# Low parts of key and value weights by subtraction on VectorE, pooling sums emitted between keys and values, late modulation moved among the pairs and behind the weighted scores

## The chip, the cores and the metric

The kernel runs on one core of one Trainium2 chip. The metric is the device time of one execution in microseconds (us). The kernel before takes 945.13 us, the median of three runs (944.65 to 946.53).

A core has engines that run in parallel, each with its own in-order list of instructions: TensorE (PE in the profile; its weight loads are PEld) multiplies matrices, VectorE (DVE) and ScalarE (ACT) work on vectors, GpSimd (POOL) does little arithmetic here but issues some transfers, and SyncE (SP) issues the other transfers. Transfers (DMA) move data between the large memory and the on-chip memory. One engine waits for another, or for a transfer, through semaphores.

## The reference

One layer of a hybrid diffusion backbone, for 512 latent tokens and 256 context tokens of width 1024, all in float32:

```
mod = silu(c) @ w_ada + b_ada            # six rows: shift, scale, gate, twice
a   = rmsnorm(x) * norm * (1 + scale1) + shift1      # latent and context tokens
p   = a @ w_in                           # pooling input u, q, k, v, output gate, two branch gates, 16 mLSTM gates
pool = ((window_mean(u, 2/4/8/16) - u) @ w_pool[g]) * pool_scale       # four groups, on an 8 x 64 grid
q, k = silu(short_conv(q, k))            # three taps along the tokens
h    = mlstm(q, k, v, gates) forward + backward      # four heads of 256, chunks of 128, start state from the context
m    = rmsnorm(h) * gain * sigmoid(o)
y    = sigmoid(g5) * pool + sigmoid(g6) * m
x    = x + gate1 * (y @ w_out)
x    = x + gate2 * swiglu(rmsnorm(x) * norm * (1 + scale2) + shift2)
out  = rmsnorm(x) * norm
```

The last four rows of `mod` (gate1, shift2, scale2, gate2) are needed only from `y @ w_out` on.

## The kernel before

**How a product is made.** A float32 matrix is held as two matrices of type float32r: a high part (the value rounded by a cast) and a low part (the value minus the high part). `mm3` (L186) forms each product from three matmuls, high by high (L190), high by low of the activations (L191), low of the weights by high (L192). Every weight that is used has to be loaded, cast (ScalarE) and given a low part before L192 can run. `wload` (L150) does this: it loads the weight into a staging tile `wr` (three buffers), casts it to `wh` on ScalarE (L156) and makes `wl`. `wh` and `wl` have two buffers each, so the cast of one weight waits until the matmuls of the weight two before have read theirs.

**Two ways to the low part.** With no destination given, VectorE subtracts: `wl = wr - wh` (L158). With the destination `"added"`, ScalarE writes the negated weight, rounded, into `wl` (L160), and GpSimd then issues a second transfer of the same weight out of the large memory, which adds it onto `wl` on its way (L161). `keys(h)` for heads 1 to 3 (L591) and `values(h)` for heads 1 to 3 (L711, through `vload`, L194) take this second way: two weights of 512 KB each per call, twelve in all. The pooling pairs and the feed-forward have a similar transfer of their own (L238), which the change leaves alone.

**The stages.** The first 60 us prepare modulation and the normed tokens `aT` and `acT`. Then values of head 0, and the stage of the pairs (`Pool`, a subclass of `Seven`): eight times a pair of 128-column weight blocks, the pooling input and its gate, is multiplied by seven products in place of eight. Its step for pair j has a `front`, in which four of the products run, a `prepare` of pair j+1, which loads two weight blocks (`wr`, `ur`) and forms sums and low parts, and a `back` for pair j-1. `back` calls `later` and `done`, which store results (`td`, `ud`) for later use.

Then the four heads. For each head h the order in the program before is: (from head 1 on) `values(h)`, `attention(h)`, `queries(h+1)`, the rest of attention, `both_pooled(h)`, `keys(h+1)`, `mixed(h)`. For the last head `both_pooled(3)` stands ahead of `values(3)`. `attention` runs twice (two halves of the latent tokens) through `scores` (L938: products of keys and queries, weighted by decays on VectorE and split again into high and low) and `apply` (L978: products of the weighted scores with the values). `pooled` (L603) reads back a pooling input tile (`pa`, one buffer), and sums it over windows by additions on VectorE through `pb` (two buffers), scales by a loaded count table (L639, L643) and subtracts. `pool_mix` (L647) multiplies the result by the pooling weights. `mixed` joins the branches. After head 3 follow the output projection and the feed-forward.

**Late modulation.** The 32 column blocks of `mod` that are needed late are not matmuls. `late_mod(n, behind, among)` (L681) loads n blocks of 512 KB each of `w_ada` and forms each block's sum by one VectorE instruction (L687), which is held in VectorE's order behind a given instruction. With `among` it takes a `wr` buffer, otherwise a `pb` buffer, the ones that `pooled` uses. Before, the 32 blocks stand at: one per pair (8), one behind each token tile of values for heads 1 to 3 (18), and one behind each half of attention in heads 0 to 2 (6).

**What sets the order.** The first stage and part of the feed-forward are ordered by hand. Everywhere else a planner orders each engine's list, from its own cost estimates, and gives earlier places in the program priority. Each engine then runs its list strictly in that order, and so does each queue of transfers: one that waits for a buffer holds back those behind it. PSUM banks for products rotate through four tiles `ps` and four `pat`.

Of the kernel before, what the change touches and what calls it, by code (L numbers as in the profile page):

```python
# [49 lines left out]
def layer_kernel(ctx: ExitStack, tc, xT, cT, w0, w1, wv0, wv, wada_a, wada_b, par, crow, bg, wpool,  # L50
# [99 lines left out]
    def wload(src, n, dst=None, skip=0):  # L150

        raw = tl("wr", [P, WMAX], F32, 3)
        nc.sync.dma_start(raw[:, :n], src)
        if dst is None or dst == "added":
            wh, wl = (tl(t, [P, WMAX], F32R, 2, LINE)[:, skip:skip + n] for t in ("wh", "wl"))
            nc.scalar.copy(wh, raw[:, :n])  # L156
            if dst is None:
                V.tensor_sub(wl, raw[:, :n], wh.bitcast(F32))  # L158
            else:
                nc.scalar.activation(wl, raw[:, :n], AF.Copy, scale=-1.0)  # L160
                nc.gpsimd.dma_start(wl, src, accum_op=ALU.add)  # L161
            return [(wh[:, i * P:(i + 1) * P], wl[:, i * P:(i + 1) * P]) for i in range(n // P)], wh, wl
# [13 lines left out]
        return parts, None, None  # L176

    def split(src, h, l):
        nc.scalar.copy(h, src)  # L179
        V.tensor_sub(l, src, h.bitcast(F32))  # L180
        return h, l
# [11 lines left out]

    def vload(src, n, i, dst=None):  # L194

        _, wh, wl = wload(src[:, i * 4 * n:(i + 1) * 4 * n], 4 * n, dst, min(NEXT, WMAX - 4 * n))
        return [(wh[:, c * n:(c + 1) * n], wl[:, c * n:(c + 1) * n]) for c in range(4)]
# [388 lines left out]
    def keys(h):  # L586
# [3 lines left out]
        for dk in range(2):  # L590
            w = wload(w1[K0 + 2 * h + dk], D, "added" if h else "Sp")[0]  # L591
            acc, acc2 = PS(), PS()
# [115 lines left out]
    def values(h, wp=None):  # L708
        n = DH + NG if h == 0 else DH
        if wp is None:  # L710
            wp = vload(wv[h - 1], n, 0, "added") + vload(wv[h - 1], n, 1, "added")  # L711
        vh = tl("vh", [P, NTOK, DH + 2], F32R)
# [5 lines left out]
        for i, half in ((2, 0), (3, 0), (4, 0), (2, 1), (3, 1), (4, 1), (5, 0), (5, 1), (0, 0), (0, 1), (1, 0), (1, 1)):  # L718
# [15 lines left out]
            nc.scalar.copy(vh[:, i, :DH], acc[:, :DH])  # L734
            low = V.tensor_sub(vl[:, i, :DH], acc[:, :DH], vh[:, i, :DH].bitcast(F32))
            if h:
                late_mod(1, low)
        return vh, vl
# [110 lines left out]
    class Pool(Seven):  # L849
# [6 lines left out]
        def later(self, j, s, y, q):  # L856
            tanh_half(s[:, TC:], y)
            nc.sync.dma_start(td[j], s)
            late_mod(1, self.sub, True)

# [69 lines left out]
    def attention(h, qs, ks, vals, gt, fill):  # L930
# [7 lines left out]
        def scores(th, dec):  # L938
# [3 lines left out]
            for pr in (0, 1, 2):  # L942
# [9 lines left out]
                for d in range(2):  # L952
# [21 lines left out]
                    for e, t, c in where:  # L974
                        parts[d][2 * pr + e][t] = (Sh[:, c:c + P], Sl[:, c:c + P])
            return parts

        def apply(th, parts):  # L978
# [26 lines left out]
            c2 = slice(2 * th, 2 * th + 2)  # L1005
            done = V.tensor_scalar(ss[:, c2], ss[:, c2], 1.0 / DH, EPS, ALU.mult, ALU.add)
# [3 lines left out]
            late_mod((1, 1, 1, 0)[h], done)  # L1010
            return th, hs
# [64 lines left out]
    for h in range(H):  # L1076
        if h == 0:
            k_ = keys(0)
            gt = next(gen)
            q_ = queries(0)  # L1080
        else:
            if h == H - 1:
                pp = both_pooled(h)
            v = values(h)
        rest = attention(h, q_, k_, v, gt, mgate(3 + h))
        if h < H - 1:
            q_ = queries(h + 1)
            rest()
            pp = both_pooled(h)
            k_ = keys(h + 1)  # L1090
        else:
            for n in ("att", "kqp", "vg"):
                close_pool(n)
            open_pool("late1", ("act", "oh", "ol", "gh", "gl"))
            for j in range(6):
                y_split(j)
            mgate_all(KT - 1)
            rest()
# [395 lines left out]
```

## Time and profile before

| | |
|---|---|
| time, median of 3 runs | 945.13 us |
| time of the profiled execution | 946.36 us |
| span of its instructions | 944.5 us |
| TensorE busy, share of the span | 896.0 us, 95% |
| VectorE busy | 633.9 us, 67% |
| ScalarE busy | 485.3 us, 51% |
| GpSimd busy | 93.2 us, 10% |
| mean granted TensorE clock | 0.974 |
| moved by transfers | 141.41 MB, 150 GB/s |
| stage of the pairs | about 70 to 160 us |
| heads | about 160 to 545 us |

The profile is of one execution. Its busy times count instructions that run. A line of a group or of the timeline names engine, source line, operation, the tile written, the tile read, and in square brackets the time that the engine sat idle just before and what ended it. "DMA" is the share of time that the sixteen transfer engines were busy, and "PEclk" the TensorE clock that was granted, as a share of full speed. The chain of waits follows the work that ended last back to its start.

### The profile page before, as it was taken

How to read it: one execution, taken by the hardware profiler on the slowest of the kernel's cores; microseconds unless marked ns; L12 is line 12 of the kernel's file. 1: busy time of each engine (PE TensorE's matmuls, PEld its weight loads, DVE VectorE, ACT ScalarE, POOL GpSimd, SP SyncE). 2: the span in 40 equal slices, each digit the busy share in tenths (PEclk: the TensorE clock that was granted, in tenths of full speed). 3: DMA queues.
4: the chain of work that ended last, by engine and by line, in shares of the span. 5: the costliest groups of instructions: out<-in, count | busy, mean ns of one | idle time of the engine just before them, and what ended most of it. 6: DMA issues, size and time to landing. Idle time of an engine off the chain costs nothing.

```text
span 944.5 us, 16003 instructions
## 1 busy us (share of the span) xinstructions
PE 896.0 (95%) x6218; PEld 823.1 (87%) x6218; DVE 633.9 (67%) x1231; ACT 485.3 (51%) x931; POOL 93.2 (10%) x121
## 2 busy tenths in 40 slices
PE   9999999999889987998779999999999999999997
PEld 7779999888779876997678889999889998899997
DVE  5699874676567755875777577787456754667544
ACT  4576663375354525444444645676234742566542
POOL 0001110011020102011110000011000110111000
PEclk9999999999889988998998999999999999999999
DMA  9747996331666066525553383067236652656502
GB/s 355 304 131 214 284 251 197 122 97 47 163 181 197 24 144 188 182 53 123 132 169 101 120 293 123 24 165 180 80 110 170 159 135 78 177 146 139 135 8 90
DMA packets 58125, 141.41 MB, mean 150 GB/s; under 512 B 13728, under 2 KB 18112, under 8 KB 57024
## 3 DMA queue, kind: packets, MB, share of 16 engines
q1 hardware_dynamic: 48544, 119.93, 39.8%
q0 software_dynamic: 9504, 20.45, 12.5%
q8 instruction: 49, 0.80, 0.3%
q14 instruction: 28, 0.23, 0.1%
HBM read 131.69 MB, written 8.67 MB: 149 GB/s over the span
## 4 chain that ended last, share of the span: by engine, by line
PE 68%; DMA 11%; DVE 9%; issue 6%; ACT 4%; POOL 0%; DVEq 0%; POOLq 0%; SPq 0%; ACTq 0%
PE ps L190 15%; PE ps L192 15%; PE ps L191 15%; DMA pb<-in_wada_b 3%; DMA wl<-in_w 3%; PE pat L190 3%; PE pat L191 3%; PE pat L192 3%; DMA wl<-in_wv 2%; PE pat L492 2%; PE pat L991 1%; PE pat L989 1%; PE pat L990 1%; PE ps L725 1%; DMA E<-rd 1%
## 5 line engine op out<-in xcount | busy, mean ns | idle before, releaser
L156 ACT CAST wh<-wr 128x1024 fp32r<-128x1024 f32 (+3 forms) x62 | 61.8, 1001 | 115.7 <-PE ps L191 97.2
L192 PE MATMUL ps<-a,wl 128*128 128x512 f32 (+1 forms) x240 | 92.5, 385 | 13.2 <-DMA wl<-in_w 13.2
L190 PE MATMUL ps<-a,wh 128*128 128x512 f32 (+1 forms) x240 | 92.4, 385 | 0.0
L191 PE MATMUL ps<-a,wh 128*128 128x512 f32 (+1 forms) x240 | 92.1, 384 | 0.0
L192 PE MATMUL ps<-act,wl 128*128 128x512 f32 (+1 forms) x224 | 78.0, 348 | 0.9 <-DVE wl L158 0.9
L158 DVE TENSOR_TENSOR wl<-wr,wh 128x1024 fp32r<-128x1024 f32 (+3 forms) x50 | 57.5, 1149 | 30.8 <-ACT wh L156 30.0
L190 PE MATMUL ps<-act,wh 128*128 128x512 f32 (+1 forms) x224 | 77.9, 348 | 0.2 <-DVE tmp L1219 0.2
L191 PE MATMUL ps<-act,wh 128*128 128x512 f32 (+1 forms) x224 | 77.8, 347 | 0.1
L192 PEld LDWEIGHTS ps<-a,wl 128*128 128x128 f32 x240 | 48.8, 203 | 21.4 <-DMA wl<-in_w 13.8
L725 PE MATMUL ps<-wl,a 128*128 128x256 f32 (+1 forms) x192 | 56.0, 292 | 9.7 <-DMA wl<-in_wv 8.8
L238 POOL DMA_DIRECT2D ol<-in_wffi x38 | 33.0, 876 | 256.4 <-ACT ol L237 90.3
L179 ACT CAST wh<-sg 128x1024 fp32r<-128x1024 f32 x27 | 28.4, 1051 | 57.9 <-PE pat L191 47.3
L724 PE MATMUL ps<-wh,a 128*128 128x256 f32 (+1 forms) x192 | 55.8, 291 | 1.2 <-DVE tmp L562 1.2
L726 PE MATMUL ps<-wh,a 128*128 128x256 f32 (+1 forms) x192 | 55.5, 289 | 0.0
L190 PEld LDWEIGHTS ps<-a,wh 128*128 128x128 f32 x240 | 48.8, 203 | 6.9
L191 PEld LDWEIGHTS ps<-a,wh 128*128 128x128 f32 x240 | 48.6, 203 | 6.9
L180 DVE TENSOR_TENSOR wl<-sg,wh 128x1024 fp32r<-128x1024 f32 x27 | 33.1, 1224 | 31.6 <-ACT wh L179 31.5
L190 PE MATMUL ps<-hp,gh 128*128 128x256 f32 x176 | 49.9, 283 | 1.0 <-ACT pat L274 1.0
L1342 DVE SCALAR_TENSOR_TENSOR x<-ps,lb,x 128x512 f32<-128x512 f32 (+1 forms) x32 | 19.6, 616 | 45.0 <-PE ps L192 45.0
L190 PE MATMUL ps<-hp,oh 128*128 128x256 f32 x176 | 49.3, 280 | 0.1
L192 PE MATMUL ps<-hp,gl 128*128 128x256 f32 x176 | 49.2, 280 | 0.0
L191 PE MATMUL ps<-hp,gh 128*128 128x256 f32 x176 | 49.1, 279 | 0.0
(368 smaller groups left out, 3063.6 us busy)
## 6 DMA issues: line engine op xcount, KB each, us to landing
wr<-in_w SPq DMA_DIRECT2D x34, 512.0 KB, 3.9
wr<-in_wffi SPq DMA_DIRECT2D x25, 512.0 KB, 4.0
pb<-in_wada_b SPq DMA_DIRECT2D x24, 512.0 KB, 4.3
ur<-in_wffi SPq DMA_DIRECT2D x19, 512.0 KB, 4.1
ol<-in_wffi POOLq DMA_DIRECT2D x38, 256.0 KB, 5.1
ada<-in_wada_a SPq DMA_DIRECT2D x8, 1024.0 KB, 9.3
wr<-in_wffo SPq DMA_DIRECT2D x16, 448.0 KB, 3.8
ur<-in_w SPq DMA_DIRECT2D x8, 512.0 KB, 5.6
```

The source lines that it names most:

```text
L156: nc.scalar.copy(wh, raw[:, :n])
L158: V.tensor_sub(wl, raw[:, :n], wh.bitcast(F32))
L179: nc.scalar.copy(h, src)
L180: V.tensor_sub(l, src, h.bitcast(F32))
L190: nc.tensor.matmul(dst, wh, ah, start=first and i == 0, stop=False, skip_group_check=on)
L191: nc.tensor.matmul(dst, wh, al, start=False, stop=False, skip_group_check=on)
L192: nc.tensor.matmul(dst, wl, ah, start=False, stop=last and i == n - 1, skip_group_check=on)
L238: nc.gpsimd.dma_start(l, dram, accum_op=ALU.add)
L724: nc.tensor.matmul(acc[:, :n], ah, wh, start=kk == 0, stop=False)
L725: nc.tensor.matmul(acc[:, :n], ah, wl, start=False, stop=False)
L726: nc.tensor.matmul(acc[:, :n], al, wh, start=False, stop=kk == KT - 1)
L1342: V.scalar_tensor_tensor(x1[j][:, c], acc[:, c], g2[:, j:j + 1], x1[j][:, c], ALU.mult, ALU.add)
```

## The change

- The `"added"` way is gone from `wload` and `vload`. The twelve weights of keys and values in heads 1 to 3 get their low part by the subtraction on VectorE (L158). Their second transfer and their second ScalarE pass are gone.
- The program's order in the heads: `keys(h+1)`, then `both_pooled(h)`, then `values(h+1)`, then `mixed(h)`. For the last head `both_pooled(3)` stands behind the loads and splits of the stored branches (`y_split`) and ahead of the last gate tile.
- Late modulation: two blocks per pair (16), and two behind each half's weighted scores in all four heads (16), behind the last low part that `scores` makes. None behind the values or behind `apply`.

```
--- before.py
+++ after.py
@@ -151,14 +151,10 @@
 
         raw = tl("wr", [P, WMAX], F32, 3)
         nc.sync.dma_start(raw[:, :n], src)
-        if dst is None or dst == "added":
+        if dst is None:
             wh, wl = (tl(t, [P, WMAX], F32R, 2, LINE)[:, skip:skip + n] for t in ("wh", "wl"))
             nc.scalar.copy(wh, raw[:, :n])
-            if dst is None:
-                V.tensor_sub(wl, raw[:, :n], wh.bitcast(F32))
-            else:
-                nc.scalar.activation(wl, raw[:, :n], AF.Copy, scale=-1.0)
-                nc.gpsimd.dma_start(wl, src, accum_op=ALU.add)
+            V.tensor_sub(wl, raw[:, :n], wh.bitcast(F32))
             return [(wh[:, i * P:(i + 1) * P], wl[:, i * P:(i + 1) * P]) for i in range(n // P)], wh, wl
         if dst == "wide":
             h, l = (wide(t)[:, skip:skip + n] for t in ("gh", "gl"))
@@ -175,9 +171,11 @@
             parts += [(h[:, i * P:(i + 1) * P], l[:, i * P:(i + 1) * P]) for i in range(m // P)]
         return parts, None, None
 
+    low_part = [None]
+
     def split(src, h, l):
         nc.scalar.copy(h, src)
-        V.tensor_sub(l, src, h.bitcast(F32))
+        low_part[0] = V.tensor_sub(l, src, h.bitcast(F32))
         return h, l
 
     def tsplit(src, tag):
@@ -191,9 +189,9 @@
             nc.tensor.matmul(dst, wh, al, start=False, stop=False, skip_group_check=on)
             nc.tensor.matmul(dst, wl, ah, start=False, stop=last and i == n - 1, skip_group_check=on)
 
-    def vload(src, n, i, dst=None):
-
-        _, wh, wl = wload(src[:, i * 4 * n:(i + 1) * 4 * n], 4 * n, dst, min(NEXT, WMAX - 4 * n))
+    def vload(src, n, i):
+
+        _, wh, wl = wload(src[:, i * 4 * n:(i + 1) * 4 * n], 4 * n, skip=min(NEXT, WMAX - 4 * n))
         return [(wh[:, c * n:(c + 1) * n], wl[:, c * n:(c + 1) * n]) for c in range(4)]
 
 
@@ -588,7 +586,7 @@
         ks = []
         kch, kcl = S("kq", F32R), S("kq", F32R)
         for dk in range(2):
-            w = wload(w1[K0 + 2 * h + dk], D, "added" if h else "Sp")[0]
+            w = wload(w1[K0 + 2 * h + dk], D, None if h else "Sp")[0]
             acc, acc2 = PS(), PS()
             mm3(acc[:, :TC], w, acT)
             mm3(acc2, w, aT)
@@ -708,7 +706,7 @@
     def values(h, wp=None):
         n = DH + NG if h == 0 else DH
         if wp is None:
-            wp = vload(wv[h - 1], n, 0, "added") + vload(wv[h - 1], n, 1, "added")
+            wp = vload(wv[h - 1], n, 0) + vload(wv[h - 1], n, 1)
         vh = tl("vh", [P, NTOK, DH + 2], F32R)
         vl = tl("vl", [P, NTOK, DH + 2], F32R)
         nc.gpsimd.memset(vh[:, :, DH:DH + 1].bitcast(F32), 1.0)
@@ -732,9 +730,7 @@
                 for d, j in ((0, i), (1, 1 - i if i < 2 else 7 - i)):
                     V.tensor_add(gif[:, :, d, j, :], gsrc[:, d], bsrc[:, d])
             nc.scalar.copy(vh[:, i, :DH], acc[:, :DH])
-            low = V.tensor_sub(vl[:, i, :DH], acc[:, :DH], vh[:, i, :DH].bitcast(F32))
-            if h:
-                late_mod(1, low)
+            V.tensor_sub(vl[:, i, :DH], acc[:, :DH], vh[:, i, :DH].bitcast(F32))
         return vh, vl
 
 
@@ -856,7 +852,7 @@
         def later(self, j, s, y, q):
             tanh_half(s[:, TC:], y)
             nc.sync.dma_start(td[j], s)
-            late_mod(1, self.sub, True)
+            late_mod(2, self.sub, True)
 
         def done(self, j, s, x, q):
             nc.scalar.copy(q[:, :TC], x)
@@ -973,6 +969,7 @@
                     split(St[:, :n], Sh[:, :n], Sl[:, :n])
                     for e, t, c in where:
                         parts[d][2 * pr + e][t] = (Sh[:, c:c + P], Sl[:, c:c + P])
+            late_mod(2, low_part[0])
             return parts
 
         def apply(th, parts):
@@ -1003,11 +1000,10 @@
                 nc.scalar.activation(hb[:, :DH], hh, AF.Square, accum_out=ss[:, i:i + 1])
                 hs.append(hh)
             c2 = slice(2 * th, 2 * th + 2)
-            done = V.tensor_scalar(ss[:, c2], ss[:, c2], 1.0 / DH, EPS, ALU.mult, ALU.add)
+            V.tensor_scalar(ss[:, c2], ss[:, c2], 1.0 / DH, EPS, ALU.mult, ALU.add)
             nc.gpsimd.tensor_tensor(rst[:, c2], ss[:, c2], mhalf[:, :2], ALU.pow)
             for t in range(2):
                 nc.scalar.activation(hs[t], hs[t], AF.Copy, scale=rst[:, 2 * th + t:2 * th + t + 1])
-            late_mod((1, 1, 1, 0)[h], done)
             return th, hs
 
         def turn(th, hs):
@@ -1078,22 +1074,20 @@
             k_ = keys(0)
             gt = next(gen)
             q_ = queries(0)
-        else:
-            if h == H - 1:
-                pp = both_pooled(h)
-            v = values(h)
         rest = attention(h, q_, k_, v, gt, mgate(3 + h))
         if h < H - 1:
             q_ = queries(h + 1)
             rest()
+            k_ = keys(h + 1)
             pp = both_pooled(h)
-            k_ = keys(h + 1)
+            v = values(h + 1)
         else:
             for n in ("att", "kqp", "vg"):
                 close_pool(n)
             open_pool("late1", ("act", "oh", "ol", "gh", "gl"))
             for j in range(6):
                 y_split(j)
+            pp = both_pooled(h)
             mgate_all(KT - 1)
             rest()
         mixed(h, pp)
```

More of the change, by code (lines that the diff above doesn't have):

```diff
@@ L153, in wload @@
         nc.sync.dma_start(raw[:, :n], src)
-        if dst is None or dst == "added":
+        if dst is None:
             wh, wl = (tl(t, [P, WMAX], F32R, 2, LINE)[:, skip:skip + n] for t in ("wh", "wl"))
             nc.scalar.copy(wh, raw[:, :n])
[L157 to L161, printed above, removed]
+            V.tensor_sub(wl, raw[:, :n], wh.bitcast(F32))
             return [(wh[:, i * P:(i + 1) * P], wl[:, i * P:(i + 1) * P]) for i in range(n // P)], wh, wl
@@ L1088, in layer_kernel @@
             rest()
+            k_ = keys(h + 1)
             pp = both_pooled(h)
-            k_ = keys(h + 1)
+            v = values(h + 1)
         else:
```

26 lines of the change are left out of this document (11 added, 15 removed).

## The prediction

> **What bounds the kernel now.** I read the page first (engines, then the forty slices).
>
> ```profile
> span 944.5 us, 16003 instructions
> PE 896.0 (95%) x6218; PEld 823.1 (87%) x6218; DVE 633.9 (67%) x1231; ACT 485.3 (51%) x931; POOL 93.2 (10%) x121
> ...
> PEclk9999999999889988998998999999999999999999
> DMA  9747996331666066525553383067236652656502
> ```
>
> TensorE sets the time: 95% busy, and its clock dips in slices 11 to 22 alone, the heads. So I asked for the busy times of stretches: the pairs, the heads, then the places behind each long wait.
>
> ```profile
> core 0: us, PE busy (x) PEld busy (x) DVE busy (x) ACT busy (x) POOL busy (x), PEclk, DMA share, GB/s
> 90.00:145.00 55.00, 55.00 (x475) 55.00 (x475) 44.48 (x73) 34.89 (x67) 9.63 (x11) 1.00 0.96 269
> 230.00:500.00 270.00, 233.83 (x1417) 209.51 (x1416) 178.40 (x359) 125.25 (x247) 31.77 (x41) 0.92 0.52 140
> ...
> 241.00:248.00 7.00, 6.71 (x28) 6.39 (x29) 1.70 (x4) 0.62 (x1) 0.00 (x0) 0.55 0.77 204
> 269.00:275.00 6.00, 5.69 (x28) 5.69 (x29) 1.97 (x2) 3.61 (x11) 0.73 (x2) 0.53 0.95 236
> 337.00:344.00 7.00, 6.62 (x29) 6.31 (x30) 2.17 (x4) 0.62 (x1) 0.00 (x0) 0.58 0.92 214
> 366.00:373.00 7.00, 6.38 (x42) 6.38 (x43) 5.41 (x7) 5.69 (x14) 2.31 (x3) 0.76 0.73 182
> 436.00:443.00 7.00, 6.97 (x30) 6.56 (x31) 2.57 (x4) 0.62 (x1) 0.94 (x1) 0.58 0.87 213
> 494.00:504.00 10.00, 7.73 (x36) 7.07 (x37) 8.88 (x16) 4.55 (x13) 1.01 (x2) 0.66 0.50 164
> ```
>
> In 230 to 500 us TensorE idles 270 - 233.8 = 36.2 us and runs at 0.92 of its clock: 0.08 x 270 = 21.6 us more. These 57.8 us are the prize. Elsewhere little is lost; in the pairs nothing, but there the transfer engines are 0.96 busy. Next, TensorE's waits from 160 to 560 us.
>
> ```profile
> PE ps L192 <- DMA wl<-in_w: 13.2, 3, 4.5
> PE ps L725 <- DMA wl<-in_wv: 8.8, 4, 2.9
> PE ps L190 <- DVE tmp L562: 3.6, 2, 3.4
> PE pat L991 <- DVE Sp L180: 2.5, 3, 1.4
> PE pat L989 <- ACT Sp L179: 2.5, 2, 2.2
> PE pat L951 <- DVE kq L180: 1.9, 2, 1.5
> ```
>
> The first two rows are the transfers that add low parts: 22.0 us in seven waits. Five of these seven are followed by the slow clock, in the first five short stretches above: 0.45 x 7 + 0.47 x 6 + 0.42 x 7 + 0.24 x 7 + 0.42 x 7 = 13.5 us. Together 35.5 us.
>
> The rows for Sp, 5.0 us, lie near 490 to 498 us. There the chain of waits runs through late modulation:
>
> ```profile
> 484.84 3.84 DMA pb<-in_wada_b
> 488.70 1.24 DVE pb L687 x2
> 489.96 4.86 DMA pb<-in_wada_b
> ```
>
> Six blocks share two buffers, VectorE stands at each until it has landed, and the scores of head 3 stand behind. With 0.34 x 10 = 3.4 us of clock that is 8.4 us. The rest of the prize, 57.8 - 35.5 - 8.4 = 13.9 us, is waits of keys and pooling on VectorE (the rows L562 and kq) and their clock.
>
> **The change part by part.** *Low parts.* One weight of keys(1), from ScalarE's timeline and the chain of waits:
>
> ```profile
> 230.56 1.05 ACT L156 CAST wh<-wr 128x1024 fp32r<-128x1024 f32 x1 [0.29 <-PE ps L191]
> 232.19 1.05 ACT L160 ACTIVATE wl<-wr 128x1024 fp32r<-128x1024 f32 x1
> 233.54 7.71 DMA wl<-in_w
> ```
>
> From the cast's start to the landed low part: 241.25 - 230.56 = 10.7 us. TensorE ran out of work at 233.5. The subtraction in its place, from VectorE's timeline:
>
> ```profile
> 288.72 1.22 DVE L158 TENSOR_TENSOR wl<-wr,wh 128x1024 fp32r<-128x1024 f32 x1 [0.41 <-ACT wh L156]
> ```
>
> Cast and subtraction take 1.05 + 1.22, some 2.4 us: ready at 232.9, before TensorE needs it. Removed: twelve passes of ScalarE (12.6 us, off the path), twelve issues of GpSimd, 6.3 MB of transfers. Added: 12 x 1.22 = 14.6 us of VectorE in the heads, beside TensorE's work; the 35.5 us go. Cover: a cast waits for the matmuls of the weight two before, so a low part is hidden by the work of one weight. A keys weight has 24 matmuls of 256 columns and 24 of 512; a piece of the chain of either kind:
>
> ```profile
> 475.95 0.12 PE ps L725
> ...
> 232.57 0.23 PE ps L192
> ```
>
> That is 24 x 0.35 = 8.4 us of cover for keys. The second half of values has less: 36 matmuls of 256 columns stand ahead of its first use, 4.2 us. That leaves 1.8 us for VectorE's list, in which conversion of keys and sums of pooling now stand. Bounds per head change: below, 0; above, the longest wait of VectorE for a count table in front of a pooling instruction:
>
> ```profile
> 247.18 0.69 DVE L643 TENSOR_TENSOR tmp<-pb,tmp 128x512 f32<-128x512 f32 x1 [4.58 <-DMA tmp<-in_icnt]
> ```
>
> 4.58 - 1.8 = 2.8 us, and 2.9 us of clock behind it as in the stretches above, 5.7 us. I take 2 us, nearer the lower end: most low parts are not behind such an instruction. Three times, once per change of head: +6 (0 to 17).
>
> *Order of keys, pooling, values.* The conversion of keys no longer stands behind pooling sums, and 144 matmuls of values (17 us) lie ahead of pooling's product, so the 13.9 us should shrink. No row shows what other waits come up; bounds: all or nothing of it. I take half: -7 (0 to -14). For the last head the pooling sums move from about 445 to 488 us to the end of attention, where only the last gate tile (48 matmuls of 512, 11 us) covers them. Its transfers also stand behind six loads of stored branches on SP's queue. What one tile takes there: the load of the chain, then the first and the last of its VectorE instructions.
>
> ```profile
> 458.95 5.76 DMA pa<-ud
> ...
> 482.63 0.48 DVE L631 TENSOR_TENSOR pb<-pa 128x316 f32<-128x316 f32 x1
> 487.18 0.68 DVE L180 TENSOR_TENSOR pm<-tmp,pm 128x512 fp32r<-128x512 f32 x1
> ```
>
> 5.8 + 5.2 = 11 us for a tile, of which there are two with one buffer between them: 22 us. Nothing but the planner's liking keeps them from starting within attention, as the stored input has long been there. I take +2, nearer the lower end for that; the ends are 0 and 22 - 11 = 11.
>
> *Late modulation in the heads.* Eighteen blocks leave the values, six leave the places behind attention, sixteen come behind scores, two at a time with over 20 us between, so both buffers have landed. The 8.4 us go. Behind each pair stand the reciprocals of `apply`, which waits 2 x 1.22 = 2.4 us longer, eight times; gate and query tiles fill TensorE meanwhile. +2 (0 to 2.4 x 8 = 19, if no fill is left).
>
> *Late modulation among the pairs.* Eight blocks more. VectorE's own period there, and the transfers from 100 to 145 us:
>
> ```profile
> 124.80 1.23 DVE L180 TENSOR_TENSOR wl<-sg,wh 128x1024 fp32r<-128x1024 f32 x1 [1.83 <-ACT wh L179]
> 134.56 1.23 DVE L180 TENSOR_TENSOR wl<-sg,wh 128x1024 fp32r<-128x1024 f32 x1 [1.83 <-ACT wh L179]
> q1 hardware_dynamic: 3259, 9.48, 61.5%
> q0 software_dynamic: 1440, 2.62, 35.0%
> ...
> wr<-in_wada_b SPq DMA_DIRECT2D x6, 512.0 KB, 5.2
> ```
>
> A pair takes 9.76 us. VectorE has 44.48 / 55 of that, 7.9 us, and gets 1.3 us: covered, barely, by the 1.83 us hole. The ordinary queue moved 9.48 MB in 0.615 x 45 us, 342 GB/s, so 0.52 MB more costs 1.5 us of transfer engines per pair: 0.96 x 9.76 + 1.5 = 10.9 us against 9.76. Some six pairs are that full: 6 x 1.15 = 7 us, less what prefetch and the light slices at both ends take up. Besides, three tiles per pair now rotate through three `wr` buffers where there were two: the next weight can load only once this one has been read. Its first and last read on ScalarE, and the landing of all tiles `wr` from 60 to 240 us:
>
> ```profile
> 116.79 0.62 ACT L233 CAST oh<-wr 128x512 fp32r<-128x512 f32 x1
> 119.77 0.63 ACT L237 ACTIVATE ol<-wr 128x512 fp32r<-128x512 f32 x1
> ...
> DMA to landing us min/median/max: 2.7/4.9/8.1
> ```
>
> From first to last read 120.4 - 116.8 = 3.6 us, with 5.2 us to land 8.8 us: it just fits 9.76. I take +5 (0, if prefetch holds; 16, if landing grows to its longest, 8.1 us: 8 x 2.0).
>
> [...] The rows show 0.96 busy at 269 GB/s, so I keep +5.
>
> [...]
>
> **Sum**, against the profiled execution's 946.4 us (span 944.5 and 1.9 around it): -35.5 - 8.4 - 7 + 6 + 2 + 2 + 5 = -35.9, so 910.5. The profiled execution stands 1.2 us above the median of 945.1; against that, 909. I say 910.
>
> **The rivals.** (1) *The pairs become bound by transfers or buffers.* The three rows on landing and reading speak for it, eager prefetch and idle transfer slices at 145 to 165 us against. +16 for +5: 921, and with the slow clock behind four of these waits (2.9 each) 933.
>
> (2) *The waits change their name.* VectorE is 178.4 of 270 us busy in the heads; with 14.6 more and eight blocks fewer (9.8) it has 183 us of work in some 225 (270 less 57.8, plus the new waits), 0.81. If the six weights at the head changes still wait half as long as now, 17.7 of the 35.5 return: 928. For it: VectorE's 4.58 us stand. Against: that stand cost TensorE nothing, and keys have 8.4 us of cover.
>
> (3) *Slower: low parts stuck in VectorE's list.* If the planner places the twelve behind pooling instructions that wait for transfers, each stalls TensorE. The net of all other terms is -35.9 - 6 = -41.9; so it decides from 41.9 / 12 = 3.5 us each, clock included. For keys that means a list 8.4 - 2.4 + 3.5 = 9.5 us long ahead of the subtraction. At 4.58 us each, the wait for the count table: 946.4 - 41.9 + 55 = 959. Against: there is one such table per pooled tile, two per head, and four low parts.
>
> (4) *Nothing new appears.* All 57.8 us go, no term is added: 889.
>
> (5) *It doesn't do what it says*: pooling sums still delay keys, as the planner orders by its own costs. Then -7 is 0: 917, inside the forecast's own range.
>
> **How the numbers follow.** Forecast with (5), 900 to 921: 0.50. (1) 0.13, (2) 0.19, (3) 0.10, (4) 0.08. The likeliest is 910. The range, 895 to 938, takes in (1), (2) and part of (4): about 0.8. About 0.2% (1.9 us) can be told from no change here. Faster is all but (3) and a worse (2): 0.86; same 0.03; slower 0.11.
>
> **What would show it.** Right: no "DMA wl" among TensorE's waits; idle under 12 us and clock over 0.97 from 230 us to the last head's end; no Sp wait near a pb block. In the pairs: period up to 10.3 us, landing of `wr` above 5.2 us; wrong if TensorE stays full there. Wrong in the heads: PE waits named "DVE wl L158" over 2 us each, above all at L725; at the end, "pm" waits ahead of the output projection.

## The result, and the profile after

The changed kernel takes 906.71 us, the median of four runs (904.8 to 907.49). The kernel before takes 945.19 us beside it (four runs, 944.65 to 946.53). The ratio is 0.9588, with a 95% interval of 0.9569 to 0.9607. The forecast was 910, its range 895 to 938. The profiled execution took 906.13 us, 40.2 us less than the one of before (946.36).

The page of the changed kernel, engines and slices:

```profile
span 904.4 us, 15980 instructions
...
PE 880.4 (97%) x6218; PEld 810.7 (90%) x6218; DVE 640.7 (71%) x1243; ACT 474.1 (52%) x919; POOL 78.9 (9%) x109
...
PEclk9999999999999999999999899999999999999999
```

The dips of the clock in slices 11 to 22 are gone but for one, in slice 23, near the end of the heads. The stretches that answer to those of before, then two at the end of head 3 (columns: length, busy time of each engine with its instructions, granted clock, share of the transfer engines, GB/s):

```profile
90.00:145.00 55.00, 52.68 (x452) 52.48 (x452) 48.90 (x81) 33.65 (x65) 9.61 (x11) 1.00 1.00 301
230.00:500.00 270.00, 262.49 (x1680) 236.40 (x1678) 202.90 (x424) 139.27 (x289) 21.56 (x32) 0.99 0.38 117
490.00:500.00 10.00, 6.54 (x28) 4.72 (x26) 8.08 (x17) 5.01 (x8) 0.62 (x1) 1.00 0.54 177
500.00:510.00 10.00, 7.61 (x23) 5.68 (x23) 6.80 (x10) 4.56 (x7) 0.00 (x0) 0.66 0.34 99
```

In the heads TensorE idles 7.5 us of 270 where it idled 36.2, and the clock rises from 0.92 to 0.99. Two losses are new: 2.3 us in the pairs, and the idle time and slow clock of the last two rows. TensorE's waits from 160 to 560 us were headed by transfers; this is the head of the list after, from 60 to 560 us (total, times, longest):

```profile
PE ps L188 <- ACT pm L177: 3.5, 2, 1.9
PE ps L188 <- ACT pat L272: 2.3, 1, 2.3
PE ps L190 <- DVE wl L157: 2.0, 3, 1.2
PE ps L188 <- ACT wh L156: 1.8, 1, 1.8
PE pat L988 <- DVE Sp L178: 1.4, 3, 0.6
```

No transfer stands in it. (Lines have moved: the subtraction of a weight's low part is now L157, the three matmuls L188 to L190, late modulation L683 and L685.)

**A ledger of lost time.** To compare kernels I count, in each, what TensorE loses between 60 and 560 us: its idle time, and what the slow clock takes, (1 - clock) x 10 us summed over stretches of 10 us. These rows carry the idle part, first of the kernel before:

```profile
60.00:180.00 120.00, 118.55 (x937) 114.83 (x937) 90.80 (x179) 70.91 (x136) 14.80 (x17) 1.00 0.78 226
230.00:480.00 250.00, 218.55 (x1312) 195.62 (x1311) 162.51 (x324) 115.94 (x224) 30.35 (x39) 0.92 0.52 138
480.00:560.00 80.00, 75.17 (x424) 65.41 (x423) 55.03 (x122) 39.20 (x84) 2.83 (x4) 0.96 0.51 163
```

and of the changed one:

```profile
60.00:180.00 120.00, 116.21 (x924) 112.75 (x923) 98.99 (x194) 70.31 (x135) 14.78 (x17) 1.00 0.87 261
230.00:480.00 250.00, 245.94 (x1608) 223.48 (x1607) 187.87 (x390) 127.26 (x266) 20.24 (x30) 0.99 0.37 114
480.00:560.00 80.00, 74.15 (x463) 66.21 (x462) 55.98 (x114) 43.52 (x87) 3.16 (x4) 0.96 0.45 149
```

The same for the kernels of the experiments below (us, idle + clock; the sum has 0.1 more, from 180 to 230 us):

| kernel | 60 to 180 | 230 to 480 | 480 to 560 | sum | ratio to before, 95% interval |
|---|---|---|---|---|---|
| before | 1.5 + 0 | 31.4 + 18.7 | 4.8 + 3.4 | 59.9 | 1 |
| changed | 3.8 + 0 | 4.0 + 1.7 | 5.8 + 3.4 | 18.9 | 0.9588 (0.9569 to 0.9607) |
| subtraction alone | 1.5 + 0 | 12.5 + 5.1 | 0 | 19.1 | 0.9594 (0.9568 to 0.9621) |
| changed, low parts added again | 4.7 + 1.7 | 32.8 + 18.7 | 7.2 + 3.4 | 68.6 | 1.0045 (1.0021 to 1.0069) |
| changed, order undone | 4.7 + 1.7 | 7.4 + 5.1 | 0.1 + 0 | 19.1 | 0.9575 (0.9548 to 0.9601) |
| changed, late modulation undone | 1.7 + 0 | 17.9 + 7.5 | 8.8 + 4.4 | 40.4 | 0.9821 (0.9792 to 0.985) |
| changed, pooling ahead of the splits | 4.7 + 1.7 | 2.8 + 0 | 2.8 + 1.7 | 13.7 | 0.9572 (0.9538 to 0.9605) |

The ledger falls by 41.0 us from before to changed, where the span fell by 40.1; in the other rows of this table it agrees with the spans within 3.4 us. So the time went where the forecast looked, into TensorE's idle time and clock. Later stages end the heads sooner in the faster kernels, so 480 to 560 us holds the last head's scores before the change, and the end of attention and the output projection after it.

### The profile page after: what moved, and what is told of

The parts are those of the page before. It is cut to its first block, busy times and chain, and to the rows that moved or that the text cites. A ratio compares the mean times of both kernels' runs of the same rounds, so it can differ in the third digit from the quotient of the medians.

```text
span 904.4 us, 15980 instructions
## 1 busy us (share of the span) xinstructions
PE 880.4 (97%) x6218; PEld 810.7 (90%) x6218; DVE 640.7 (71%) x1243; ACT 474.1 (52%) x919; POOL 78.9 (9%) x109
## 5 line engine op out<-in xcount | busy, mean ns | idle before, releaser
L157 DVE TENSOR_TENSOR wl<-wr,wh 128x1024 fp32r<-128x1024 f32 (+3 forms) x62 | 72.8, 1175 | 34.3 <-ACT wh L156 33.6
L188 PE MATMUL ps<-a,wh 128*128 128x512 f32 (+1 forms) x240 | 88.8, 370 | 0.0
L189 PE MATMUL ps<-a,wh 128*128 128x512 f32 (+1 forms) x240 | 88.7, 370 | 0.0
L190 PE MATMUL ps<-a,wl 128*128 128x512 f32 (+1 forms) x240 | 88.6, 369 | 0.0
L188 PE MATMUL ps<-act,wh 128*128 128x512 f32 (+1 forms) x224 | 78.7, 351 | 1.9 <-ACT wh L156 1.8
L190 PE MATMUL ps<-act,wl 128*128 128x512 f32 (+1 forms) x224 | 78.4, 350 | 0.9 <-DVE wl L157 0.9
L722 PE MATMUL ps<-wh,a 128*128 128x256 f32 (+1 forms) x192 | 54.3, 284 | 0.0
L724 PE MATMUL ps<-wh,a 128*128 128x256 f32 (+1 forms) x192 | 54.3, 283 | 0.0
L190 PEld LDWEIGHTS ps<-a,wl 128*128 128x128 f32 x240 | 45.2, 189 | 7.2
L189 PEld LDWEIGHTS ps<-a,wh 128*128 128x128 f32 x240 | 45.3, 189 | 6.9
L188 PEld LDWEIGHTS ps<-a,wh 128*128 128x128 f32 x240 | 45.3, 189 | 6.8
L188 PE MATMUL ps<-hp,gh 128*128 128x256 f32 x176 | 50.2, 285 | 1.0 <-ACT pat L272 1.0
L188 PEld LDWEIGHTS ps<-act,wh 128*128 128x128 f32 x224 | 42.7, 191 | 7.9 <-ACT wh L156 2.3
L188 PE MATMUL ps<-hp,oh 128*128 128x256 f32 x176 | 49.2, 279 | 0.1
L190 PE MATMUL ps<-hp,gl 128*128 128x256 f32 x176 | 49.1, 279 | 0.0
```

Source lines behind the costliest of these rows:

```text
L188: nc.tensor.matmul(dst, wh, ah, start=first and i == 0, stop=False, skip_group_check=on)
L189: nc.tensor.matmul(dst, wh, al, start=False, stop=False, skip_group_check=on)
L190: nc.tensor.matmul(dst, wl, ah, start=False, stop=last and i == n - 1, skip_group_check=on)
L722: nc.tensor.matmul(acc[:, :n], ah, wh, start=kk == 0, stop=False)
L724: nc.tensor.matmul(acc[:, :n], al, wh, start=False, stop=kk == KT - 1)
```

## The experiments

All ratios are to the kernel before, run beside each on the same chip; "by ratio" means times 945.2 us.

**Subtraction alone.** The kernel before, with the twelve low parts subtracted on VectorE and nothing else changed.

```diff
-            if dst is None:
-                V.tensor_sub(wl, raw[:, :n], wh.bitcast(F32))
-            else:
-                nc.scalar.activation(wl, raw[:, :n], AF.Copy, scale=-1.0)
-                nc.gpsimd.dma_start(wl, src, accum_op=ALU.add)
+            V.tensor_sub(wl, raw[:, :n], wh.bitcast(F32))
...
-            w = wload(w1[K0 + 2 * h + dk], D, "added" if h else "Sp")[0]
+            w = wload(w1[K0 + 2 * h + dk], D, None if h else "Sp")[0]
...
-            wp = vload(wv[h - 1], n, 0, "added") + vload(wv[h - 1], n, 1, "added")
+            wp = vload(wv[h - 1], n, 0) + vload(wv[h - 1], n, 1)
```

> The kernel before with the first part of the change alone: the twelve low parts of keys and values by subtraction on VectorE, order and late modulation as before. Theory A (each part gains what its own waits cost, the parts add up): the 22.0 us of waits for added low parts and the 13.5 us of slow clock behind them go, up to 6 us of new waits on VectorE come: 910 to 916 us, no wait of TensorE named DMA wl, the waits for Sp near the pb blocks stay. Theory B (the parts pay only together, since in the old order VectorE's list holds low parts behind pooling sums): 925 us or more, with waits of TensorE on DVE wl over 2 us each.

It took 907.53 us (907.35 to 908.63), 906.8 by ratio: the whole gain of the change, and the interval is nearly the same. TensorE's waits in this kernel, and its last stretch:

```profile
PE ps L186 <- DVE tmp L558: 6.0, 2, 4.7
PE pat L987 <- DVE Sp L176: 2.2, 4, 0.9
...
230.00:480.00 250.00, 237.53 (x1526) 214.11 (x1525) 202.33 (x405) 122.99 (x255) 24.28 (x30) 0.98 0.44 133
480.00:560.00 80.00, 80.00 (x530) 73.51 (x529) 55.20 (x114) 45.62 (x92) 2.54 (x3) 1.00 0.48 158
```

The waits on conversions and pooling (tmp) are still there, one of them longer (4.7 us where 3.4 was the longest). But the loss at the scores of head 3, 8.2 us in the ledger, has shrunk to 2.9 us of Sp waits with no dip behind them, though the late modulation there was not touched. So the three parts don't pay only together, and the other two do not add the 6.4 us that were forecast for them: the two ratios differ by 0.0006, 0.6 us, with intervals of 1.8 and 2.5 us either way.

**Low parts added again.** The changed kernel with the old way to the low parts, new order and new places of late modulation kept.

```diff
-            V.tensor_sub(wl, raw[:, :n], wh.bitcast(F32))
+            if dst is None:
+                V.tensor_sub(wl, raw[:, :n], wh.bitcast(F32))
+            else:
+                nc.scalar.activation(wl, raw[:, :n], AF.Copy, scale=-1.0)
+                nc.gpsimd.dma_start(wl, src, accum_op=ALU.add)
...
-            w = wload(w1[K0 + 2 * h + dk], D, None if h else "Sp")[0]
+            w = wload(w1[K0 + 2 * h + dk], D, "added" if h else "Sp")[0]
...
-            wp = vload(wv[h - 1], n, 0) + vload(wv[h - 1], n, 1)
+            wp = vload(wv[h - 1], n, 0, "added") + vload(wv[h - 1], n, 1, "added")
```

> The changed kernel with the first part undone: low parts of keys and values again by the adding transfer, new order and new places of late modulation kept. Theory A: the 35.5 us come back less what the new order hides of them: 935 to 943 us, waits of TensorE for DMA wl of 15 to 22 us. Theory B: the waits come back only in part, 918 to 930 us.

It took 950.29 us (948.38 to 951.79), a little slower than before and above both ranges. Its longest waits:

```profile
PE ps L727 <- DMA wl<-in_wv: 16.8, 6, 5.5
PE ps L194 <- DMA wl<-in_w: 14.5, 3, 5.1
```

31.3 us, where before they were 22.0. All six low parts of values are late now, by up to 5.5 us; in the new order the values stand right behind the pooling sums and their loads. Against the changed kernel the old low parts cost (1.0045 - 0.9588) x 945.2 = 43.2 us: more than the 38.4 us that removing them alone gained. What in the new order makes them later was not tried by itself.

**Keys alone.** The kernel before with the six weights of keys subtracted, those of values still added.

```diff
-            w = wload(w1[K0 + 2 * h + dk], D, "added" if h else "Sp")[0]
+            w = wload(w1[K0 + 2 * h + dk], D, None if h else "Sp")[0]
```

> The kernel before with the low parts of the six weights of keys subtracted on VectorE; those of the values stay added by transfer. Theory, by the prediction's split of the 35.5 us: three waits of keys, 13.2 us, and three of the slow stretches behind them, 3.2 + 2.8 + 2.9 = 8.9 us: 945 - 22 = 923 us, with the waits of the values at 8.8 us as before. Rival: the waits of the values grow when those of keys go, as they grew from 8.8 to 16.8 us when the low parts were added in the new order: 928 to 935 us.

927.91 us (927.18 to 928.8); ratio 0.9823 (0.979 to 0.9855), 16.7 us less than before and 928.5 by ratio. The time is in the rival's range, but not by its cause:

```profile
PE ps L725 <- DMA wl<-in_wv: 8.1, 3, 2.8
PE ps L190 <- DVE tmp L562: 5.4, 2, 4.2
PE pat L991 <- DVE Sp L180: 4.3, 4, 1.8
```

The waits of values did not grow (8.1 us for 8.8). The keys' 13.2 us and their clock went, and part came back as waits on VectorE: on tmp 5.4 for 3.6 us, on Sp 4.3 for 2.5. TensorE reaches the pooling products and the scores earlier, and VectorE's list is not ready. The values' six weights then bring the other 38.4 - 16.7 = 21.7 us, where I had 35.5 - 22.1 = 13.4 for them. So, taken in this order, the keys were worth less than their own waits, the values more.

**No blocks behind the values, in the kernel before.** The eighteen blocks are neither loaded nor multiplied; their columns of `mod` stay zero.

```diff
-            low = V.tensor_sub(vl[:, i, :DH], acc[:, :DH], vh[:, i, :DH].bitcast(F32))
+            V.tensor_sub(vl[:, i, :DH], acc[:, :DH], vh[:, i, :DH].bitcast(F32))
             if h:
-                late_mod(1, low)
+                next(late)
```

> The kernel before without the eighteen blocks behind the values, which are not computed (their columns of the modulation stay zero); everything else as before, the added low parts too. Theory of the prediction, by which the late modulation in the heads had a price of its own of 8.4 us (most of it before the scores of the last head): some 936 us. Rival: the waits there are hidden behind, or made by, the waits for transfers, so little is gained while these last: 942 to 945 us. If more than 8.4 us go, late modulation was part of the cause of the slow low parts too.

936.61 us (932.21 to 939.19); ratio 0.9912 (0.9877 to 0.9947), 8.3 us less (5.0 to 11.6), as forecast. In this kernel TensorE loses almost nothing from 480 us on, where it lost 8.2:

```profile
480.00:560.00 80.00, 79.16 (x472) 69.61 (x471) 56.46 (x119) 44.63 (x92) 2.99 (x4) 1.00 0.44 149
```

So the reading of the profile before was right as far as it went: the blocks cost some 8 us there. The subtraction removes most of the same loss by another way. What the two traces show of that way: before, the loads of the blocks are issued at 484.84 us, when the last pooling sum has freed the `pb` buffers, and the scores are due at 490; with the subtraction they are issued at 451.32, and from 455 to 460 us TensorE has 23 matmuls of a gate tile beside them, where before it has only a few from 490 to 495. That the gate tile is what covers the blocks was not tested by itself.

**Late modulation undone.** The changed kernel with the blocks of late modulation at their old places.

```diff
-            V.tensor_sub(vl[:, i, :DH], acc[:, :DH], vh[:, i, :DH].bitcast(F32))
+            low = V.tensor_sub(vl[:, i, :DH], acc[:, :DH], vh[:, i, :DH].bitcast(F32))
+            if h:
+                late_mod(1, low)
...
-            late_mod(2, self.sub, True)
+            late_mod(1, self.sub, True)
...
-            late_mod(2, low_part[0])
...
+            late_mod((1, 1, 1, 0)[h], done)
```

> The changed kernel with the third part undone: late modulation once per pair, once behind each token tile of values, once behind each half of attention in heads 0 to 2. Theory A: the 8.4 us of head 3 come back, the one wait of 2.3 us in the pairs goes, in the other heads up to 3 us: 910 to 916 us. Theory B (late modulation was hidden anyway): 903 to 906 us, only the pairs' 2.3 us change.

928.31 us (927.43 to 931.63), ratio 0.9821: in the new order the old places cost 22.0 us against the changed kernel, far more than forecast. The longest waits, GpSimd's instruction behind the first, and SP's queue ahead of it (its waits from 355 to 378 us, then two of its issues):

```profile
PE pat L987 <- POOL tmp L902: 9.8, 2, 5.6
PE ps L188 <- ACT pm L177: 6.8, 2, 5.6
...
383.12 0.73 POOL L902 TENSOR_TENSOR tmp<-E,maskF 128x256 f32<-128x256 f32 x1 [16.92 <-DMA E<-rd]
...
SPq L683 <- DVE pb L685: 7.1, 4, 2.8
...
373.15 0.33 SPq L683 DMA_DIRECT2D pb<-in_wada_b  x1
...
375.06 0.43 SPq L898 DMA_DIRECT2D E<-rd  x1
```

`E`, the decays that the scores are weighted with, is loaded by SP's queue, behind loads of blocks; four of these wait, 7.1 us in all, until VectorE's sum of an earlier block frees one of the two `pb` buffers. It is issued at 375.06; GpSimd, which applies the mask, has been idle for 16.92 us when it lands, and TensorE waits 5.6 us for what follows. In the changed kernel, at the same place in head 2:

```profile
362.14 0.52 SPq L896 DMA_DIRECT2D E<-rd  x1
```

**The same, without the eighteen blocks behind the values.**

```diff
             if h:
-                late_mod(1, low)
+                next(late)
```

> The run with the late modulation undone (928.3 us), without the eighteen blocks behind the values: these are not computed, so their columns of the modulation stay zero; six blocks behind attention and one per pair stay. Theory: what cost 21.6 us there was the loads of those blocks, which wait on SP's queue for one of two buffers and hold the loads of stored heads (E<-rd) behind them; without them 904 to 908 us, and no TensorE wait of over 2 us for the tmp of L902's kind. Rival: the new order of keys, pooling and values itself makes the waits, and the blocks only fill VectorE: 18 x 1.2 = 22 us of VectorE fewer, little of it on the path: 920 to 928 us.

899.67 us (896.18 to 901.56), ratio 0.9519 (0.9484 to 0.9554), 899.7 by ratio: 28.5 us less than with the blocks. The time is below the range that was forecast. `E` is issued at 356.60 us, and no wait of TensorE is over 2.1 us:

```profile
PE ps L188 <- ACT pm L177: 2.1, 1, 2.1
...
356.60 0.57 SPq L899 DMA_DIRECT2D E<-rd  x1
```

The new order itself makes no such waits. The blocks do, and in the old order with added low parts the same eighteen cost 8.3 us. How much of the 28.5 us is the queue and how much the blocks' time on VectorE (18 x 1.2 us) isn't separated by this run, and a full kernel has to spend that time somewhere; of the longest waits above, the longer of the two behind `tmp`, 5.6 of 9.8 us, is the queue's.

**Order undone.** The changed kernel with the old order of keys, pooling and values.

```diff
+        else:
+            if h == H - 1:
+                pp = both_pooled(h)
+            v = values(h)
...
-            k_ = keys(h + 1)
             pp = both_pooled(h)
-            v = values(h + 1)
+            k_ = keys(h + 1)
...
-            pp = both_pooled(h)
```

> The changed kernel with the second part undone: pooling sums ahead of keys, values behind mixed, the last head's pooling sums ahead of its values, as before. Theory A: the waits of pooling and keys come back (13.9 us with their clock), the 9 us at the last head's end (490 to 504 us of the changed kernel) go: 908 to 914 us. Theory B: 920 us or more, with waits of TensorE for DVE wl at the values.

905.28 us (904.4 to 907.6), ratio 0.9575: the same as the changed kernel within the intervals, and below the range that was forecast. Its ledger tells why. The heads lose 12.5 us where the changed kernel loses 5.7, and the end loses 0.1 where that loses 9.2. The new order gains some 7 us in the heads and gives them back at the end. The pairs, which this edit leaves alone, lose 2.6 us more in this execution than in the changed kernel's; the sums are equal only with that.

**The last head's pooling sums, ahead of the splits.** First the place of the loss. In the changed kernel, SP's queue and TensorE at the end of head 3:

```profile
474.46 11.15 SPq L1048 DMA_DIRECT2D tmp<-yd  x6
485.90 0.33 SPq L637 DMA_DIRECT2D tmp<-in_icnt  x1
...
491.78 0.53 SPq L618 DMA_DIRECT2D pa<-ud  x1
...
491.73 0.73 PE L188 MATMUL ps<-pm,wh 128*128 128x512 f32 x2 [1.59 <-ACT pm L177]
499.33 0.73 PE L188 MATMUL ps<-pm,wh 128*128 128x512 f32 x2 [1.86 <-ACT pm L177]
503.70 0.79 PE L188 MATMUL ps<-act,wh 128*128 128x512 f32 x1 [1.84 <-ACT wh L156]
```

The six loads of stored branches take their turn on SP's queue over 11.15 us, the count tables come behind them, the second tile waits for the one `pa` buffer until 491.78, and its product starts at 499.33. So the sums are put ahead:

```diff
+            pp = both_pooled(h)
...
             for j in range(6):
                 y_split(j)
-            pp = both_pooled(h)
```

> The changed kernel with the last head's pooling sums emitted just ahead of the loads and splits of the stored branches, not behind them. Theory A (the idle 5.9 us and 3.4 us of slow clock at 490 to 504 us of the changed kernel come from the count tables and the second pooling tile, which stand on SP's queue behind six loads of stored branches): the waits for pm go, 897 to 900 us. Theory B (VectorE has no room for the sums inside attention, and something else becomes late): 903 to 908 us.

903.39 us (901.55 to 904.76), ratio 0.9572; the ledger of the end falls from 9.2 to 4.5 us. So the place on SP's queue makes about half of that loss; one pm wait of 2.8 us stays. The time, 904.7 by ratio, lies in the range of theory B and can't be told from the changed kernel's. A variant puts them ahead of attention, where they stood before:

```diff
+        if h == H - 1:
+            pp = both_pooled(h)
         rest = attention(h, q_, k_, v, gt, mgate(3 + h))
...
-            pp = both_pooled(h)
```

> The changed kernel with the last head's pooling sums emitted ahead of its attention, behind mixed of head 2. Theory A: as the run before, 897 to 900 us. Theory B (sums with priority over the scores delay them, as VectorE holds its list): 901 to 906 us, with waits of TensorE for Sp in head 3.

906.99 us (902.27 to 908.4), ratio 0.9602 (0.9562 to 0.9643). The profiled execution is its fastest (902.27). In it the pooling waits go and one of 4.0 us inside attention, on ScalarE, takes their place: no gain.

**Blocks per pair.** Three kernels ask what two blocks in each pair cost. In the changed kernel there is one stall, at 114.04 us. The chain back from it, on VectorE, ScalarE and TensorE, and the issue on SP's queue that it hangs on:

```profile
105.72 1.22 DVE L685 SCALAR_TENSOR_TENSOR wr<-wr,crow_s 128x1024 f32<-128x1024 f32 x1 [2.71 <-DMA wr<-in_wada_b]
...
109.55 0.62 ACT L231 CAST oh<-wr 128x512 fp32r<-128x512 f32 x1 [1.98 <-DMA wr<-in_w]
...
114.04 0.38 PE L188 MATMUL ps<-hg,gh 128*128 128x256 f32 x1 [2.32 <-ACT pat L272]
...
102.76 0.33 SPq L225 DMA_DIRECT2D wr<-in_w  x1
```

VectorE stands 2.71 us for a block, ScalarE 1.98 us for a weight that was issued at 102.76. After it TensorE stays full to 150 us. First, one block per pair and three behind each pair of scores:

```diff
-            late_mod(2, self.sub, True)
+            late_mod(1, self.sub, True)
...
-            late_mod(2, low_part[0])
+            late_mod(3, low_part[0])
```

> The changed kernel with one block of late modulation per pair and three behind each half's scores. Theory C (transfers bound the pairs, as forecast at +5 us): the pairs win their one wait of 2.3 us, no more, and the third block behind the scores waits for one of two buffers with VectorE standing at it and loads behind it on SP's queue: 908 to 918 us. Theory D (blocks behind scores are hidden): 903 to 906 us.

907.51 us (906.11 to 911.59), ratio 0.9624 (0.9585 to 0.9662): 909.7 by ratio. The stall is gone, the heads hide the third block (4.5 us in the ledger), and the end grows from 9.2 to 11.1 us, with one pm wait of 4.8. Nothing is gained. Second, three per pair and one behind the scores:

```diff
-            late_mod(2, self.sub, True)
+            late_mod(3, self.sub, True)
...
-            late_mod(2, low_part[0])
+            late_mod(1, low_part[0])
```

> The changed kernel with three blocks of late modulation per pair and one behind each half's scores. Theory C (342 GB/s is what the transfer engines give in the pairs, each further block costs 1.5 us of them): 12.4 us per pair against 9.76, 915 to 928 us. Theory D (the busy share is no limit, more bytes go through at the same share; buffers and VectorE, 9.2 us of work per pair with two blocks and 10.5 with three, set the period): 10.5 us per pair, 909 to 914 us.

927.84 us (926.67 to 930.4), ratio 0.9837 (0.9795 to 0.9878): (0.9837 - 0.9588) x 945.2 = 23.5 us slower than with two. The time is in the range of theory C, but not by its cause. Its stretch of the pairs, ScalarE's read of a weight in two pairs, and the longest wait of SP's queue from 90 to 150 us:

```profile
90.00:150.00 60.00, 52.64 (x400) 51.07 (x398) 40.60 (x71) 25.11 (x50) 6.98 (x8) 0.91 0.84 260
...
135.11 1.14 ACT L231 CAST oh<-wr 128x512 fp32r<-128x512 f32 x2 [2.64 <-DMA wr<-in_w]
149.68 1.14 ACT L231 CAST oh<-wr 128x512 fp32r<-128x512 f32 x2 [3.41 <-DMA wr<-in_w]
...
SPq L683 <- DVE sg L255: 21.2, 5, 6.1
```

A pair takes 149.68 - 135.11 = 14.6 us where it took 9.76. Neither the transfer engines (0.84, 260 GB/s) nor VectorE (40.6 of 60 us) is full. Four tiles pass through three `wr` buffers in each pair, and SP's queue stands 21.2 of the 60 us with the load of a block until VectorE's last read of a weight (`sg`) frees one. That points to the buffers; a run with a fourth `wr` buffer, which would show it directly, was not made. The losses run on to 230 us, where the pairs end later.

**Both cures.** Pooling sums ahead of the splits, one block per pair, three behind the scores: the edits of two kernels above in one.

> The changed kernel with the last head's pooling sums ahead of the splits of the stored branches (as in the run of that name, 903.4 us), one block per pair instead of two, and three behind each pair of scores instead of two. Theory: the pairs' one stall (2.3 us before the copy of L272 in the changed kernel) goes, as it did with one per pair, and the tail does not grow, since its sums no longer stand behind the splits: 903.4 - 2.3 to 3.1 = about 900.5 us, no PE wait for the copy of a pair above 1 us, pm waits before the output projection at most 3 us in sum. Rival: the third block behind scores delays the pooling sums of the last head again (5.8 us of pm waits in the run with one per pair): 904 to 907 us.

903.61 us (901.59 to 907.97), ratio 0.9573 (0.9543 to 0.9604): 904.8 by ratio, in the rival's range and no better than the early sums alone. The pairs' stall is gone (1.5 us in the ledger for 6.4), the end grows from 4.5 to 8.7. TensorE's product with the second pooling tile, first with early sums alone, then with both:

```profile
494.25 0.73 PE L188 MATMUL ps<-pm,wh 128*128 128x512 f32 x2 [2.80 <-ACT pm L177]
```

```profile
494.32 0.79 PE L188 MATMUL ps<-pm,wh 128*128 128x512 f32 x1 [5.32 <-ACT pm L177]
```

The tile is ready at the same time, to 0.1 us; TensorE comes 2.5 us earlier and waits as much longer. What the pairs give back is lost there, 4.2 us, and in the heads, which lose 2.4 us more behind the third block.

## Why the prediction was right, and where by chance

The sum was -35.9 us and the profiled executions differ by -40.2. By stage, forecast against the ledger:

| | forecast | measured |
|---|---|---|
| heads (-35.5 - 8.4 - 7 + 6 + 2) | -42.9 | 58.3 to 5.7: -52.6 |
| pairs (+5) | +5 | +2.3 |
| end of the last head (+2) | +2 | 0 to 9.2: +9.2 |

The heads came out 9.7 us better and the end 7 us worse, and these two errors largely covered each other. That the total is off by so little is in part luck.

**Low parts, -35.5: right in size, and alone the whole result.** All seven waits on transfers are gone, and the subtraction alone gains 38.4 us. Its ledger closes on the forecast's terms: it falls by 59.9 - 19.1 = 40.8 us, and that is the 35.5 and the 5.3 by which the loss at the scores shrank (8.2 to 2.9). The split of the 35.5 between keys and values was not right: the keys alone gave 16.7 for 22.1. One row was misread: TensorE did not run out of work at 233.5 us, where the chain passes to the transfer's issue, but at 236.9, 4.42 us ahead of 241.29; the terms don't use it.

**Late modulation, -8.4, and order, -7: true losses, but no separate gains.** The step that failed is the addition. Without its eighteen blocks behind the values the kernel before gains 8.3 us, as read. (VectorE stood less at them than was said: it idles 2.2 us in all before the six blocks; their sums, 1.2 us each, take more.) With subtraction most of that loss has gone already, and by ratio the two parts move the time together by -0.6 us, where -6.4 (-8.4 - 7 + 2 + 2 + 5) was forecast. They aren't independent of each other either: with the subtraction, the new order alone costs 21.5 us, the new places alone gain 1.8, which is within the intervals, and in the new order the new places are worth 22.0. In the heads the two do what was said and more (17.6 us lost with the subtraction alone, 5.7 with all). The end and the pairs take it back, 9.2 + 2.3.

**New waits for low parts, +6: too much.** TensorE waits 2.0 us for `wl`, in three waits of at most 1.2 us, and none of them is at the values of heads 1 to 3, where I had put them. **Blocks behind the scores, +2:** Sp waits of 1.4 us in all, none by a `pb` block.

**End of the last head, +2: too little; the bound of 11 held.** I took the lower end because nothing but the planner's liking kept the sums from starting in attention. SP's queue kept them: the six loads ahead of the count tables, which I had named and then set aside, make 4.7 of the 9.2 us, as the sums ahead of the splits show.

**Pairs, +5: wrong in kind, 2.3 in size.** I took 0.96 of busy transfer engines for 0.96 of their capacity and reckoned 10.9 us per pair. Behind the one stall the period stayed (9.76 us from 127.86 to 137.62), and from 90 to 145 us the share rose to 1.00 while 12% more was moved in the same time, 301 GB/s for 269. Transfers from 100 to 145 us, after, and the landing of all `wr` tiles from 60 to 240 us:

```profile
DMA packets 5157, 14.10 MB, mean 313 GB/s; under 512 B 575, under 2 KB 575, under 8 KB 5152
...
DMA to landing us min/median/max: 3.5/5.5/7.6
```

Before, 0.96 went with 269 GB/s; here, from 100 to 145 us, 313 GB/s pass in the same engines.

**The clock.** I counted slow clock behind waits of 2 to 3 us. The end shows it behind shorter ones: waits of 1.86 and 0.55 us, then 0.50 from 501.6 to 508.5 us, with the wait of 1.84 us in it; that is the 0.66 from 500 to 510 us.

**Rivals.** (1) bounds in the pairs: one stall instead of a longer period; with a third block the period grows, and SP's queue stands at the buffers. (2) waits that change name: not at the six weights, which I had in mind, but at the end, by 9.2 us. (3) slower: no low part stood long in VectorE's list. (4) nothing new: the heads nearly went that way, 5.7 us left. (5) the order does what it says: it moves 7 us out of the heads.

## What to carry to other kernels

Waits that stood one behind another in the same in-order lists could not be added up here as gains of several edits: with the first removed, the other two parts moved the time by -0.6 us where -6.4 was forecast. Measure or reckon each edit in the state that the others leave, as here, where one of three parts held the whole gain. When work is moved, read the queue that it is moved behind: here a load that waited for a buffer held those behind it on SP's queue, and that made waits of up to 5.6 us in the heads, with late modulation undone, and about half of the 9 us at the end. A busy share of transfer engines near 1 did not say that they were full: 0.96 went with 269 GB/s, 1.00 with 301 (90 to 145 us).

## What was not expected of the hardware

**Waits of 0.36 to 0.64 us were followed by a slow clock.** In the changed kernel, TensorE's only waits from 280 to 290 us are three short ones within 3 us, and the clock falls behind them (the last two rows are stretches of 2 us; the next has 1.00 again):

```profile
287.26 0.36 PE L986 MATMUL pat<-vh,Sp 128*128 128x258 f32 x1 [0.36 <-POOL tmp L900]
288.38 0.39 PE L988 MATMUL pat<-vh,Sp 128*128 128x258 f32 x1 [0.64 <-DVE Sp L178]
289.79 0.43 PE L988 MATMUL pat<-vh,Sp 128*128 128x258 f32 x1 [0.42 <-DVE Sp L178]
...
290.00:292.00 2.00, 2.00 (x11) 2.00 (x11) 2.00 (x6) 1.49 (x5) 0.00 (x0) 0.50 0.14 41
292.00:294.00 2.00, 2.00 (x13) 2.00 (x13) 2.00 (x3) 2.00 (x7) 0.00 (x0) 0.65 0.75 83
```

(0.50 + 0.35) x 2 = 1.7 us are lost for 1.42 us of idle time: the clock stands at 0.50 for 3.4 us, from 290.0 to 293.4. The single stall of 2.32 us at 114 us lost none (the ledger has 0 there). The same stall is 2.4 us with the sums ahead of attention and costs no clock; it is 2.6 us with the order undone and 3.1 with the sums ahead of the splits, and 1.7 us of clock go with each. In most places the loss was 1.7 or 3.4 us and not in proportion to the wait: 3.4 behind the end's waits of under 2 us, 3.4 behind one of 5.32 us with both cures, 1.7 behind one of 2.80 us with the early sums. At the end of the changed kernel the clock stands at 0.50 for 6.8 us, from 501.6 to 508.5, twice the 3.4 us above for twice the 1.7 us. What sets off a slow stretch, no run here isolates.
